# Closing attention by a transposed reciprocal, and a new cost model in the instruction planner, in a hybrid RWKV-7 / gMLP / attention backbone

## The chip, the cores and the metric

One Trainium2 chip, one core. The metric is the device time of one launch in microseconds, the median of several runs. The engines are TensorE (PE, with PEld for its weight loads), VectorE (DVE), ScalarE (ACT), GpSimd (POOL) and SyncE (SP, which issues the DMAs).

## The reference

Two layers over 512 latent tokens and 256 context tokens of width 1024. In each layer one input projection feeds three groups of heads (RWKV-7 in two directions, a chunked spatial gate, grouped-query attention with 6 query heads), one output projection and a SwiGLU follow, each with adaLN modulation and a gated residual. What the change rewrites is the end of the attention:

```python
def _attend(q, keys, vals):
    s = jnp.einsum('bqhgd,bkhd->bhgqk', q, keys).astype(jnp.float32) * (HEAD_DIM ** -0.5)
    p = jax.nn.softmax(s, axis=-1).astype(vals.dtype)
    return jnp.einsum('bhgqk,bkhd->bqhgd', p, vals)
...
    o = lax.map(lambda qblk: _attend(qblk, k_all, v_all), qb)
    ...
    if need_ctx_out:
        ...
        oc = _attend(qc, kc, vc).reshape(qc.shape[:2] + (C_W,))
    ...
    x = x + g1 * (jnp.concatenate([oA, oB, oC], axis=-1) @ w_out)
    x = x + g2 * swiglu(modulate(rmsnorm(x, n2), sh2, sc2), w1, w2)
```

The context queries (`oc`) exist in the first layer only. Everything is float32. The scan of the RWKV heads and the attention don't depend on each other; both end in the concatenation before `w_out`.

## The kernel before

Activations lie with the channels on the partitions and the tokens along the free dimension. Matrices are split into a high and a low part, and a product is three matmuls. Each layer has an input part (norm, 20 chunks of the input projection), a **planned part** (the method `rwkv`) and a feed-forward part. In the profile the planned part of the first layer runs from about 263 to 745 us, that of the second from about 1472 to 1900 us.

In the planned part nine generators run side by side: `scan(0)` and `scan(1)` (the recurrences, 9 units of 4 chunks each in either direction), `stage2` (inverses, by `inverse`), `solve` (a substitution on POOL between two DMAs), `back`, `front` (preparing units), `pairs`, `post` (the output norm of the RWKV heads) and `project`. `project` runs the whole attention first, then the output projection (tiles `o_ps`). `interleave` draws the next step from the generator that the planner's running clock puts earliest, which fixes the order of emission and with it the order in which buffers of a ring are handed out.

When all is emitted, `Planner.order` sorts the instructions anew. `graph` builds the dependencies, `cost` gives every instruction a duration and a lag (`late`), `HOPS` the delay from engine to engine. `run` is a list scheduler with priorities, run forward and backward in turn for `ROUNDS` rounds with the settings in `WEIGHTS`; it also guesses when TensorE's clock is halved (`active`, `ACTIVE`, `slow`). The round with the shortest modelled span wins, and its order is written into PE, DVE, ACT and POOL as a chain of dependencies, so each of these engines runs its instructions strictly in that order. SP is not ordered. `cost` puts a DVE instruction at 69 ns and 1.04 ns for each column (reciprocals too), and an ACT one that reads PSUM at 50 ns and 0.85 ns for each column.

Attention works by items: 6 heads of 512 latent queries, and in the first layer also 6 heads of 256 context queries, so 12 items and then 6. Of an item, `att_max` finds bounds of the scores, `att_scores` makes one block of transposed scores (`st_ps`, in the PSUM ring "as" of two buffers) and its exponentials (`p`, in a ring of one buffer, and `ph`), `att_rest` their low part `pl`, and `att_weigh` adds the block's product with the values to `o` (tile `at_ps`, a ring of one). The values stand beside 64 columns of ones, so `o` holds the output in one half of the partitions and the sum of the exponentials, repeated 64 times, in the other. `att_close` divides:

```python
        y = self.mix[5 + it["j"]][pr, q0:q0 + nq]
        self.nc.vector.reciprocal(out=y, in_=o[op, :nq])
        self.tt(y, o[pr, :nq], y, ALU.mult)
```

The next item's first product can't enter `at_ps` until both have read it.

Of the kernel before, what the change touches and what calls it, by code (L numbers as in the profile page):

```python
# [8 lines left out]
F32 = mybir.dt.float32  # L9
F32R = mybir.dt.float32r  # L10
AF = mybir.ActivationFunctionType
ALU = mybir.AluOpType
# [6 lines left out]
TL = 512  # L19
# [23 lines left out]

WEIGHTS = ((60.0, 0.0), (60.0, 0.15), (20.0, 0.15), (120.0, 0.3), (20.0, 0.4), (8.0, 0.15))
DRAIN = (0.10, 0.14)
ACTIVE = 3400
TICK = 10.24 / 3
SOON = 3.0
ROUNDS = 40
LATE = (0.0, 0.0, 0.4, 0.2, 0.6, 0.3, 0.5, 0.4, 1.0)  # L50


ENGINES = ("PE", "DVE", "Activation", "Pool", "SP")

HOPS = {("Activation", "PE"): 0.25, ("DVE", "PE"): 0.23, ("PE", "Activation"): 0.2, ("PE", "DVE"): 0.2,
        ("DVE", "Activation"): 0.13, ("Activation", "DVE"): 0.15, ("Activation", "Pool"): 0.17, ("DVE", "Pool"): 0.12,
        ("Pool", "Activation"): 0.08, ("Pool", "DVE"): 0.08, ("Pool", "PE"): 0.2, ("PE", "Pool"): 0.22}

# [12 lines left out]
class Planner:  # L71
# [25 lines left out]
    def cost(self, i, e):  # L97

        out = i.outs[0].bass_ap
        n = 1  # L100
        for _, k in out.ap[1:]:
            n *= k
        ins = [a.bass_ap for a in i.ins if hasattr(a, "bass_ap")]
        late = 0.0
        if e == "PE":
            m, rows = out.ap[0][1], ins[0].ap[0][1]
            low = out.offset // out.ap[0][0] == 0
            dur, occ, load, passes = n / 2.4, 0.0, m / 1.2, 1
            if i.is_transpose:
                dur, load, passes = dur * 2, load / 2, 2  # L110
            elif i.ins[0].dtype == F32:
                dur, passes = dur * 4, 4
                if not low or rows <= 64 < m:
                    dur, late = dur / 2, dur / 2
                if low:
                    occ = m / 1.2

            shape = tuple(32 if x <= 32 else 64 if x <= 64 else 128 for x in (rows, m))
            self.parts[i.name] = (dur + 2) / 1e3, (occ + 2) / 1e3, load / 1e3, n * passes * rows / 128, shape
            c = max(dur, occ + load) + 2  # L120
        elif e == "DVE":
            kind = type(i).__name__
            wide = len([a for a in ins if len(a.ap) > 2 or a.ap[-1][1] > 1])
            if kind == "InstTensorReduce":
                for _, k in ins[0].ap[1:]:
                    n *= k
                c = 40 + 1.04 * n
            elif kind == "InstMemset" or kind in ("InstTensorScalarPtr", "InstTensorCopy") and wide < 2 and \
                    not any(a.tensor.name in self.psum for a in ins):
                c = 69 + 0.52 * n  # L130
            else:
                c = 69 + 1.04 * n + (60 if len(ins) > 2 else 0)
        elif e == "Activation":
            c = (50 if ins[0].tensor.name in self.psum else 57) + 0.85 * n + 95 * (len(ins) - 1)
        elif e == "Pool":
            if str(getattr(i, "op", "")).endswith("pow"):
                c = 400 + 165 * n
            elif not ins:
                c = 130 + 0.85 * n
            else:  # L140
                c = 250 + 2.1 * n if n > 100 else 260 + 1.65 * n
        else:
            c = 2700 + (0.6 * n if out.ap[0][1] == 128 else 0)
        return c / 1e3, late / 1e3
# [95 lines left out]
    def order(self):  # L240

        ins = [i for i in self.bb.instructions[self.from_:] if i.is_executable and len(i.outs)]
        eng = [str(i.engine).split(".")[-1] for i in ins]
        n = len(ins)
        deps, data, ready = self.graph(ins, eng)
        cost, late = zip(*[self.cost(i, e) for i, e in zip(ins, eng)])
        parts = [self.parts.get(i.name) for i in ins]

        def lag(j, k):
            if eng[j] == eng[k] and eng[j] in ("DVE", "Activation"):  # L250
                return 0.12 if j in data[k] else 0.0
# [8 lines left out]
        def run(prio, back, weight=(60.0, 0.0)):  # L260

            wait_w, stay = weight
            pre, suc = (succ, pred) if back else (pred, succ)
            left = [len(p) for p in pre]
            at = [0.0] * n if back else list(ready)
# [5 lines left out]
            start, seq = [0.0] * n, []  # L271
            loaded, active, shape, end = 0.0, {}, None, 0.0
            while len(seq) < n:
# [5 lines left out]
                if e == "PE" and not back:  # L279
# [4 lines left out]
                    drain = DRAIN[slow > 1.0]  # L284

                    def delay(k):
                        if parts[k][4] == shape:
                            return max(0.0, loaded + slow * parts[k][2] - t)
                        return max(0.0, end + drain - t) + slow * parts[k][2]

                    k = max(av, key=lambda k: prio[k] - wait_w * delay(k))
                    if stay and parts[k][4] != shape:

                        soon = [r for r, x in pend[e] if r < t + stay and parts[x][4] == shape and prio[x] > prio[k] - wait_w * stay]
                        if soon:
                            free[e] = min(soon)
                            continue
                    dur, occ, load, cols, form = parts[k]
                    if form != shape:
                        t = max(t, end + drain)  # L300
                        f = t + slow * (load + dur)
                    else:
                        t = max(t, loaded + slow * load)
                        f = t + slow * dur
                    loaded, end, shape = t + slow * occ, f, form
                    active[int(f / TICK)] = active.get(int(f / TICK), 0.0) + cols
                else:
# [24 lines left out]
            return start, seq, max(free.values())  # L332

        prio = [0.0] * n
# [50 lines left out]
class Kern:  # L385
# [323 lines left out]
    def attention(self, pool, psp, tn):  # L709
# [12 lines left out]
        for n, _ in enumerate(items):  # L722
# [1111 lines left out]
```

## Time and profile before

| what | us |
|---|---|
| median of 3 runs | 2278.98 (2271.74 to 2285.78) |
| the profiled execution's own time | 2289.83 |
| its span, first to last instruction | 2288.1 |
| planned part, layer 0 (263 to 745) | 482 |
| feed-forward, layer 0, with the norm before it (745 to 1307) | 562 |
| planned part, layer 1 (1472 to 1900) | 428 |
| feed-forward, layer 1, and the end (1900 to 2288) | 388 |

The profiled execution is 10.9 us above the median and 1.7 us longer than its span. The rest of the span is the two input parts. The stretches were cut by hand where the first and last instructions of a part lie, so neighbours overlap a little.

### The profile page before, as it was taken

The numbers are of one execution on the slowest core, as the hardware profiler recorded it, in microseconds if no ns is written. First come the engines' busy times: TensorE is split into PE (matmuls) and PEld (weight loads), VectorE is DVE, ScalarE is ACT, GpSimd is POOL, SyncE is SP. The second block draws the span as 40 slices with busy tenths as digits, with TensorE's granted clock in tenths as the row PEclk, the third lists the DMA queues.
The fourth block names the chain that finished last, engine by engine and source line by source line (L and its number), as shares of the span: only waits on it lengthen the run. The fifth ranks groups of instructions, "written<-read, shape, count | busy, mean of one in ns | idle before, by whom it ended". The sixth has DMA issues, their size and how long they took to land.

```text
span 2288.1 us, 37945 instructions
## 1 busy us (share of the span) xinstructions
PE 2109.2 (92%) x15184; PEld 1718.6 (75%) x15184; DVE 1343.8 (59%) x2362; ACT 871.9 (38%) x1822; POOL 475.7 (21%) x965
## 2 busy tenths in 40 slices
PE   6989988888999899999999899979888898999997
PEld 2778765666788788888888778756666777888886
DVE  3677787778646744296354464477786646333334
ACT  3534355564544421121121254336555444222221
POOL 0123372444311100000000012363534401000000
PEclk9999887987699899999999999977898898999998
DMA  7433010001211423256253231011111212323322
GB/s 262 144 119 121 30 28 10 16 19 27 61 50 36 145 92 89 68 175 191 77 175 114 100 97 56 28 21 18 23 28 30 74 49 75 101 92 96 97 91 76
DMA packets 128928, 183.05 MB, mean 80 GB/s; under 512 B 82032, under 2 KB 85360, under 8 KB 128752
## 3 DMA queue, kind: packets, MB, share of 16 engines
q1 hardware_dynamic: 128752, 180.63, 26.0%
q8 instruction: 119, 1.95, 0.4%
q14 instruction: 57, 0.47, 0.1%
HBM read 168.93 MB, written 11.67 MB: 79 GB/s over the span
## 4 chain that ended last, share of the span: by engine, by line
PE 65%; DVE 8%; ACT 4%; issue 2%; DMA 1%; POOL 1%; POOLq 0%; SPq 0%; DVEq 0%; ACTq 0%
PE pgate L413 26%; PE p L413 14%; PE g_ps L413 6%; PE o_ps L413 5%; PE sc_ps L413 4%; PE st_ps L413 2%; PE at_ps L413 1%; DVE mix L822 1%; PE pe L413 1%; DVE BK L406 1%; DVE sz L406 1%; ACT XU L400 1%; PE pT L413 1%; PE pa_ps L413 1%; PE pD L413 1%
## 5 line engine op out<-in xcount | busy, mean ns | idle before, releaser
L400 ACT ACTIVATE whi<-wraw 128x1024 fp32r<-128x1024 f32 (+1 forms) x192 | 198.2, 1033 | 727.7 <-issue 260.3
L413 PE MATMUL pgate<-h2l,whi 128*128 128x512 f32 (+1 forms) x1056 | 376.5, 357 | 4.0 <-DVE h2l L406 4.0
L413 PE MATMUL pgate<-h2h,whi 128*128 128x512 f32 (+1 forms) x1056 | 375.2, 356 | 4.2 <-ACT h2h L400 3.2
L413 PE MATMUL pgate<-h2h,wlo 128*128 128x512 f32 (+1 forms) x1056 | 376.6, 357 | 0.0
L403 DVE TENSOR_TENSOR wlo<-wraw,whi 128x1024 fp32r<-128x1024 f32 (+1 forms) x192 | 231.9, 1208 | 188.3 <-ACT whi L400 176.1
L413 PEld LDWEIGHTS pgate<-h2h,whi 128*128 128x128 f32 x1056 | 199.9, 189 | 37.2 <-ACT h2h L400 4.0
L413 PEld LDWEIGHTS pgate<-h2l,whi 128*128 128x128 f32 x1056 | 199.7, 189 | 37.2 <-DVE h2l L406 5.4
L413 PEld LDWEIGHTS pgate<-h2h,wlo 128*128 128x128 f32 x1056 | 199.6, 189 | 28.7
L403 POOL TENSOR_TENSOR rs<-ms,consts_sb 128x4 f32<-128x4 f32 (+2 forms) x51 | 71.8, 1407 | 671.0 <-DVE ms L410 613.9
L413 PE MATMUL g_ps<-hh,whi 128*128 128x512 f32 (+1 forms) x552 | 193.7, 357 | 12.0 <-ACT hh L400 7.4
L413 PE MATMUL g_ps<-hl,whi 128*128 128x512 f32 (+1 forms) x552 | 195.7, 355 | 1.0 <-POOL hl L403 1.0
L413 PE MATMUL g_ps<-hh,wlo 128*128 128x512 f32 (+1 forms) x552 | 194.2, 352 | 0.0
L413 PE MATMUL p<-tL,whi 128*128 128x512 f32 (+1 forms) x528 | 186.8, 355 | 0.0
L413 PE MATMUL p<-tH,wlo 128*128 128x512 f32 (+1 forms) x528 | 186.4, 356 | 0.0
L413 PE MATMUL p<-tH,whi 128*128 128x512 f32 (+1 forms) x528 | 186.0, 354 | 0.0
L488 DVE CUSTOM_DVE_ANT_0 ada_junk<-adaw,cb,glob 128x1024 bf16<-128x1024 f32 x128 | 165.6, 1294 | 29.7 <-DMA adaw<-in_ada_w 28.1
L406 DVE SCALAR_TENSOR_TENSOR part<-p,adav,part 128x512 f32<-128x512 f32 (+1 forms) x72 | 47.5, 661 | 179.2 <-PE p L413 179.2
L406 DVE SCALAR_TENSOR_TENSOR fe<-fe,pgate 128x768 f32<-128x768 f32 (+1 forms) x88 | 71.9, 818 | 130.1 <-PE pgate L413 129.9
L413 PEld LDWEIGHTS g_ps<-hh,whi 128*128 128x128 f32 x552 | 105.7, 193 | 30.6 <-ACT hh L400 9.5
L400 ACT ACTIVATE sw<-sz,wc 64x64 f32<-64x64 f32 x264 | 90.9, 344 | 95.0 <-DVE sz L406 75.4
L413 PEld LDWEIGHTS g_ps<-hl,whi 128*128 128x128 f32 x552 | 107.1, 194 | 16.9 <-issue 2.5
L413 PEld LDWEIGHTS g_ps<-hh,wlo 128*128 128x128 f32 x552 | 106.8, 194 | 13.6 <-issue 0.6
(282 smaller groups left out, 4262.9 us busy)
## 6 DMA issues: line engine op xcount, KB each, us to landing
wraw<-in_w SPq DMA_DIRECT2D x104, 512.0 KB, 3.4
adaw<-in_ada_w SPq DMA_DIRECT2D x80, 512.0 KB, 3.7
wraw<-in_w_in SPq DMA_DIRECT2D x40, 512.0 KB, 3.7
wraw<-in_w SPq DMA_DIRECT2D x32, 448.0 KB, 3.3
adar<-in_ada_r SPq DMA_DIRECT2D x16, 512.0 KB, 8.2
wraw<-in_w_out SPq DMA_DIRECT2D x16, 448.0 KB, 3.3
drA<-EA SPq DMA_DIRECT2D x72, 64.0 KB, 2.1
Z<-drY SPq DMA_DIRECT2D x36, 128.0 KB, 3.1
```

Source lines behind the costliest of these rows:

```text
L400: self.lastact = self.nc.scalar.activation(out=out, in_=in_, func=func, **kw).ins
L403: (eng or self.nc.vector).tensor_tensor(out=out, in0=a, in1=b, op=op)
L406: self.lastdve = self.nc.vector.scalar_tensor_tensor(out=out, in0=a, scalar=s, in1=b, op0=op0, op1=op1).ins
L413: return self.nc.tensor.matmul(out=out, lhsT=lhsT, rhs=rhs, start=start, stop=stop, **kw)
L488: nc.vector.tensor_tensor_reduce(out=junk, in0=w, in1=self.cb[i], scale=1.0, scalar=self.adab[l][:, j:j + 1], op0=ALU.mult, op1=ALU.add, a ...
L822: self.nc.vector.reciprocal(out=y, in_=o[op, :nq])
```

## The change

Two things change, both inside the planned parts.

`att_close` becomes a generator of three steps. ACT copies all 128 partitions of `o` to SBUF (`ao`, which takes the one buffer of the ring "p"). TensorE transposes `ao` in blocks of 128 queries into `ot_ps` (ring "as"), so that queries lie on the partitions; VectorE takes the reciprocal of one column of each block, 128x4 or 128x2 numbers (`rc`); TensorE transposes these columns, spread over 128, back into `ob_ps` (ring "as"); VectorE multiplies `ao` by that. An item of 512 queries adds 8 transposes, one of 256 queries adds 4.

The planner gets other numbers and a second evaluation. `cost` now takes 150 ns or more for each DVE instruction and 165 or 198 ns for an ACT one, and books part of it as a lag where all 128 partitions are written; reciprocals and scans have their own slopes. `HOPS` are shorter, PE has a lag of 165 ns. PE is modelled as two halves, into which narrow matmuls go side by side in pairs. `follow` replays a finished order, engine by engine, with a clock model at three phases; a round is rated by the mean of the three spans, and priorities start from the replay. There are 100 rounds in place of 40.

```diff
-WEIGHTS = ((60.0, 0.0), (60.0, 0.15), (20.0, 0.15), (120.0, 0.3), (20.0, 0.4), (8.0, 0.15))
+WEIGHTS = ((60.0, 0.15), (20.0, 0.4), (10.0, 0.3), (120.0, 0.3), (30.0, 0.6), (8.0, 0.15), (4.0, 0.3))
 DRAIN = (0.10, 0.14)
-ACTIVE = 3400
+ACTIVE = 3600
+PHASES = (0.0, 0.33, 0.67)
 TICK = 10.24 / 3
 SOON = 3.0
-ROUNDS = 40
+ROUNDS = 100
 LATE = (0.0, 0.0, 0.4, 0.2, 0.6, 0.3, 0.5, 0.4, 1.0)
 
 
 ENGINES = ("PE", "DVE", "Activation", "Pool", "SP")
 
-HOPS = {("Activation", "PE"): 0.25, ("DVE", "PE"): 0.23, ("PE", "Activation"): 0.2, ("PE", "DVE"): 0.2,
-        ("DVE", "Activation"): 0.13, ("Activation", "DVE"): 0.15, ("Activation", "Pool"): 0.17, ("DVE", "Pool"): 0.12,
-        ("Pool", "Activation"): 0.08, ("Pool", "DVE"): 0.08, ("Pool", "PE"): 0.2, ("PE", "Pool"): 0.22}
+HOPS = {("Activation", "PE"): 0.052, ("DVE", "PE"): 0.054, ("PE", "Activation"): 0.037, ("PE", "DVE"): 0.038,
+        ("DVE", "Activation"): 0.033, ("Activation", "DVE"): 0.033, ("Activation", "Pool"): 0.077, ("DVE", "Pool"): 0.078,
+        ("Pool", "Activation"): 0.033, ("Pool", "DVE"): 0.034, ("Pool", "PE"): 0.053, ("PE", "Pool"): 0.08}
 
 
 def overlap(a, b):
...
         ins = [a.bass_ap for a in i.ins if hasattr(a, "bass_ap")]
+        full = out.ap[0][1] == 128
+        psum = any(a.tensor.name in self.psum for a in ins)
         late = 0.0
         if e == "PE":
             m, rows = out.ap[0][1], ins[0].ap[0][1]
-            low = out.offset // out.ap[0][0] == 0
-            dur, occ, load, passes = n / 2.4, 0.0, m / 1.2, 1
+            dur, load, times = n / 2.33 + 8, m / 1.2, 1
+            passes = 1
             if i.is_transpose:
-                dur, load, passes = dur * 2, load / 2, 2
+                dur, passes = n / 1.2, 2
             elif i.ins[0].dtype == F32:
-                dur, passes = dur * 4, 4
-                if not low or rows <= 64 < m:
-                    dur, late = dur / 2, dur / 2
-                if low:
-                    occ = m / 1.2
-
+                dur, passes, times = n / 1.2 + (5 if m <= 64 else 0), 4, 2
+
+            half = None if m > 64 else int(out.offset // out.ap[0][0] >= 64)
             shape = tuple(32 if x <= 32 else 64 if x <= 64 else 128 for x in (rows, m))
-            self.parts[i.name] = (dur + 2) / 1e3, (occ + 2) / 1e3, load / 1e3, n * passes * rows / 128, shape
-            c = max(dur, occ + load) + 2
+
+            self.parts[i.name] = dur / 1e3, times, load / 1e3, n * passes * rows / 128, shape, half
+            c = max(dur, load) * times
+            if half is not None:
+                c *= 0.55
+            late = 165.0
         elif e == "DVE":
             kind = type(i).__name__
             wide = len([a for a in ins if len(a.ap) > 2 or a.ap[-1][1] > 1])
             if kind == "InstTensorReduce":
                 for _, k in ins[0].ap[1:]:
                     n *= k
-                c = 40 + 1.04 * n
-            elif kind == "InstMemset" or kind in ("InstTensorScalarPtr", "InstTensorCopy") and wide < 2 and \
-                    not any(a.tensor.name in self.psum for a in ins):
-                c = 69 + 0.52 * n
+                c = 150 + 1.04 * n
+            elif kind == "InstReciprocal":
+                c = 160 + 6.25 * n
+            elif getattr(i, "is_tensor_tensor_scan", False):
+                c = 150 + 2.1 * n
+            elif kind == "InstMemset" or kind in ("InstTensorScalarPtr", "InstTensorCopy") and wide < 2 and not psum:
+                c = 150 + 0.52 * n + 55 * (len(ins) - 1)
             else:
-                c = 69 + 1.04 * n + (60 if len(ins) > 2 else 0)
+                c = 150 + 1.04 * n + (60 if len(ins) > 2 else 0)
+            c, late = (c - 83, 83) if full else (c + 12, 0)
         elif e == "Activation":
-            c = (50 if ins[0].tensor.name in self.psum else 57) + 0.85 * n + 95 * (len(ins) - 1)
+            c = (165 if psum else 198) + 0.845 * n + 90 * (len(ins) - 1)
+            c, late = (c - 93, 93) if full else (c + 14, 0)
         elif e == "Pool":
             if str(getattr(i, "op", "")).endswith("pow"):
-                c = 400 + 165 * n
+                c, late = 400 + 165 * n, -60
             elif not ins:
-                c = 130 + 0.85 * n
+                c, late = 145 + 0.84 * n, -55
             else:
-                c = 250 + 2.1 * n if n > 100 else 260 + 1.65 * n
+                c, late = 270 + 1.9 * n, -70
         else:
-            c = 2700 + (0.6 * n if out.ap[0][1] == 128 else 0)
+            c = 2600 + (0.6 * n if full else 0)
         return c / 1e3, late / 1e3
...
         def lag(j, k):
-            if eng[j] == eng[k] and eng[j] in ("DVE", "Activation"):
-                return 0.12 if j in data[k] else 0.0
+            if eng[j] == eng[k] != "SP":
+                return max(0.0, late[j]) + 0.033 if j in data[k] and eng[j] in ("DVE", "Activation") else 0.0
             return self.hop(eng[j], eng[k]) + late[j]
...
+            weights, ends = [0.0, 0.0], [0.0, 0.0]
+            active, shape = {}, None
+
+            def place(k, t, drain, slow):
+
+                dur, times, load, _, form, half = parts[k]
+                hs = (0, 1) if half is None else (half,)
+                t = max([at[k], t] + [weights[h] for h in hs])
+                if form != shape:
+                    t = max(t, max(ends) + drain)
+                t = max([t + slow * load] + [ends[h] for h in hs])
+                last = t + (times - 1) * slow * max(dur, load)
+                return t, last + slow * dur, last, hs
+
+            def occupy(k, drain, slow, t):
+                t, f, last, hs = place(k, t, drain, slow)
+                for h in hs:
+                    weights[h], ends[h] = last, f
+                tick = int(f / TICK)
+                active[tick] = active.get(tick, 0.0) + parts[k][3]
+                return t, f
+
...
+                    issue = max(0.0, t - 0.25)
+                    k = max(av, key=lambda k: prio[k] - wait_w * (place(k, issue, drain, slow)[0] - t))
                     if stay and parts[k][4] != shape:
 
                         soon = [r for r, x in pend[e] if r < t + stay and parts[x][4] == shape and prio[x] > prio[k] - wait_w * stay]
                         if soon:
                             free[e] = min(soon)
                             continue
-                    dur, occ, load, cols, form = parts[k]
-                    if form != shape:
-                        t = max(t, end + drain)
-                        f = t + slow * (load + dur)
-                    else:
-                        t = max(t, loaded + slow * load)
-                        f = t + slow * dur
-                    loaded, end, shape = t + slow * occ, f, form
-                    active[int(f / TICK)] = active.get(int(f / TICK), 0.0) + cols
+                    half = parts[k][5]
+                    both = [k]
+                    if half is not None:
+
+                        mate = [x for x in av if parts[x][4] == parts[k][4] and parts[x][5] == 1 - half]
+                        if mate:
+                            both.append(max(mate, key=lambda k: prio[k]))
+                    f = t
+                    for x in both:
+                        start[x], fx = occupy(x, drain, slow, issue)
+                        shape = parts[x][4]
+                        f = max(f, fx)
+                        av.remove(x)
+                        seq.append(x)
+                    free[e] = f
+                    for k in both:
+                        for x, l in suc[k]:
+                            if eng[x] != "PE":
+                                at[x] = max(at[x], f + l)
+                            left[x] -= 1
+                            if not left[x]:
+                                heapq.heappush(pend[eng[x]], (at[x], x))
+                    continue
...
+        def follow(seq, phase):
+
+            rows = {e: [k for k in seq if eng[k] == e] for e in ENGINES}
+            nxt, free = dict.fromkeys(ENGINES, 0), dict(self.free0)
+            left, at = [len(p) for p in pred], list(ready)
+            rows["SP"] = []
+            weights, ends = [0.0, 0.0], [0.0, 0.0]
+            active, shape, slow = {}, None, 1.0
+            start, span = [0.0] * n, 0.0
+            able = []
+
+            def offer(e):
+                if nxt[e] < len(rows[e]):
+                    k = rows[e][nxt[e]]
+                    if not left[k]:
+                        heapq.heappush(able, (max(free[e], at[k]), k))
+
...
         best = None
         for i in range(ROUNDS):
-            start, seq, span = run(prio, False, WEIGHTS[i % len(WEIGHTS)])
+            _, seq, _ = run(prio, False, WEIGHTS[i % len(WEIGHTS)])
+            trace = [follow(seq, ph * TICK) for ph in PHASES]
+            span = sum(s for _, s in trace) / len(trace)
             if best is None or span < best[1]:
                 best = seq, span
+            start = trace[i % len(trace)][0]
             start, _, _ = run([t + c for t, c in zip(start, cost)], True)
             prio = [t + c for t, c in zip(start, cost)]
...
-            self.att_close(o, cur)
-            yield
+            yield from self.att_close(pool, psp, o, cur)
...
-    def att_close(self, o, it):
+    def att_close(self, pool, psp, o, it):
+
         hf, nq, q0 = it["hf"], it["nq"], it["q0"]
-        pr, op = slice(hf * 64, hf * 64 + 64), slice(64 - hf * 64, 128 - hf * 64)
-        y = self.mix[5 + it["j"]][pr, q0:q0 + nq]
-        self.nc.vector.reciprocal(out=y, in_=o[op, :nq])
-        self.tt(y, o[pr, :nq], y, ALU.mult)
+        pr, nb = slice(hf * 64, hf * 64 + 64), nq // 128
+        ao = pool.tile([128, TL], F32, name="ao", tag="p")
+        self.act(ao[:, :nq], o[:, :nq])
+        yield
+        tp = psp.tile([128, 4, 128], F32, name="ot_ps", tag="as", bufs=2)
+        for b in range(nb):
+            self.tr(out=tp[:, b, :], in_=ao[:, b * 128:(b + 1) * 128], identity=self.ident)
+        rc = pool.tile([128, 4], F32, name="rc", tag="rc")
+        self.nc.vector.reciprocal(out=rc[:, :nb], in_=tp[:, :nb, 64 - 64 * hf])
+        yield
+        bc = psp.tile([128, TL], F32, name="ob_ps", tag="as", bufs=2)
+        for b in range(nb):
+            self.tr(out=bc[:, b * 128:(b + 1) * 128], in_=rc[:, b:b + 1].to_broadcast([128, 128]), identity=self.ident)
+        self.tt(self.mix[5 + it["j"]][pr, q0:q0 + nq], bc[pr, :nq], ao[pr, :nq], ALU.mult)
+        yield
```

## Rows read from the trace of the kernel before

**Rows 1.** The page's first part: busy us, share of the span, instructions.

```profile
PE 2109.2 (92%) x15184; PEld 1718.6 (75%) x15184; DVE 1343.8 (59%) x2362; ACT 871.9 (38%) x1822; POOL 475.7 (21%) x965
```

**Rows 2.** Busy time by stretch: planned parts, their ends, feed-forward parts.

```profile
core 0: us, PE busy (x) PEld busy (x) DVE busy (x) ACT busy (x) POOL busy (x), PEclk, DMA share, GB/s
263.00:745.00 482.00, 428.25 (x4400) 339.98 (x4398) 343.03 (x739) 241.98 (x656) 186.90 (x450) 0.84 0.13 30
1472.00:1900.00 428.00, 366.49 (x3899) 281.15 (x3897) 296.79 (x646) 220.54 (x609) 173.14 (x432) 0.84 0.15 32
745.00:1307.00 562.00, 555.13 (x3173) 481.77 (x3174) 294.65 (x384) 127.36 (x145) 7.69 (x4) 0.99 0.38 122
...
600.00:745.00 145.00, 139.84 (x1602) 122.63 (x1600) 78.29 (x201) 59.26 (x172) 38.54 (x85) 0.94 0.18 48
1772.00:1900.00 128.00, 108.85 (x1278) 93.56 (x1278) 75.12 (x175) 58.31 (x163) 30.84 (x67) 0.89 0.20 57
...
1900.00:2288.00 388.00, 370.54 (x1600) 302.57 (x1600) 160.95 (x187) 104.64 (x131) 6.90 (x5) 0.97 0.29 92
```

**Rows 3.** The page's chain that ended last, by engine and by line.

```profile
PE 65%; DVE 8%; ACT 4%; issue 2%; DMA 1%; POOL 1%; POOLq 0%; SPq 0%; DVEq 0%; ACTq 0%
PE pgate L413 26%; PE p L413 14%; PE g_ps L413 6%; PE o_ps L413 5%; PE sc_ps L413 4%; PE st_ps L413 2%; PE at_ps L413 1%; DVE mix L822 1%; PE pe L413 1%; DVE BK L406 1%; DVE sz L406 1%; ACT XU L400 1%; PE pT L413 1%; PE pa_ps L413 1%; PE pD L413 1%
```

**Rows 4.** Groups on DVE and ACT by shape: busy us, mean ns, idle before.

```profile
L822 DVE RECIPROCAL mix<-at_ps 64x512 f32<-64x512 f32 x12 | 40.3, 3355 | 1.5 <-PE at_ps L413 1.1
L822 DVE RECIPROCAL mix<-at_ps 64x256 f32<-64x256 f32 x6 | 10.5, 1755 | 1.5 <-PE at_ps L413 1.3
L403 DVE TENSOR_TENSOR pl<-p,ph 128x512 fp32r<-128x512 f32 x78 | 57.4, 735 | 20.8 <-ACT ph L400 9.8 <-PE at_ps L413 9.0 <-ACT rz L400 0.5
L403 DVE TENSOR_TENSOR mix<-at_ps,mix 64x512 f32<-64x512 f32 x12 | 8.2, 685 | 0.2
L403 DVE TENSOR_TENSOR mx<-mx 128x4 f32<-128x4 f32 x12 | 2.0, 166 | 0.1
L1076 DVE COPY XU<-sc_ps 64x64 f32<-64x64 f32 x144 | 31.6, 219 | 21.3 <-PE sc_ps L413 18.8 <-POOL Z L1011 0.7
L400 ACT ACTIVATE ph<-p 128x512 fp32r<-128x512 f32 x78 | 49.0, 628 | 1.9
L400 ACT ACTIVATE p<-st_ps 128x512 f32<-128x512 f32 x78 | 46.5, 596 | 73.1 <-PE st_ps L413 41.4 <-DVE pl L403 16.4 <-PE pe L413 6.7
L400 ACT ACTIVATE XU<-sc_ps 64x64 f32<-64x64 f32 x144 | 31.2, 217 | 33.8 <-PE sc_ps L413 32.5
```

**Rows 5.** Busy by stretch: each of 18 reciprocals and 0.7 us behind it.

```profile
323.88:327.94 4.06, 2.88 (x51) 2.20 (x49) 4.02 (x3) 2.42 (x6) 2.72 (x9) 1.00 0.14 32
...
1772.74:1776.79 4.05, 2.91 (x43) 2.72 (x44) 4.02 (x2) 3.94 (x10) 2.45 (x9) 0.50 0.01 3
sum 63.39, PE 35.43 PEld 27.34 DVE 62.48 ACT 29.80 POOL 20.99; mean PE 1.97 PEld 1.52 DVE 3.47 ACT 1.66 POOL 1.17
```

**Rows 6.** Timeline around one reciprocal: start, us, instruction, idle before.

```profile
478.28 3.36 DVE L822 RECIPROCAL mix<-at_ps 64x512 f32<-64x512 f32 x1
...
481.68 0.68 DVE L403 TENSOR_TENSOR mix<-at_ps,mix 64x512 f32<-64x512 f32 x1
...
482.50 0.47 PE L413 MATMUL at_ps<-ph,vh 128*128 128x512 f32 x1 [1.76 <-DVE mix L403]
```

**Rows 7.** Timeline of TensorE: groups of four and of two transposes.

```profile
304.52 0.60 PE L416 MATMUL pb<-consts_sb,BK 128*128 128x128 f32 x4
1536.83 1.11 PE L416 MATMUL pb<-consts_sb,BK 128*128 128x128 f32 x4
1679.48 0.38 PE L416 MATMUL pb<-consts_sb,BK 128*128 128x128 f32 x2
1537.74 0.63 PE L416 MATMUL bc_ps<-consts_sb,nkk 128*128 128x128 f32 x2
```

**Rows 8.** Tile at_ps in either layer: min/median/max ns, first and last start.

```profile
L413 PE MATMUL at_ps<-ph,vh x48: 277/415/796, 298.7 to 574.7; 128*128 128x512 f32 x36, 128*128 128x256 f32 x12
L413 PE MATMUL at_ps<-ph,vh x36: 387/439/797, 1503.7 to 1767.7; 128*128 128x512 f32 x36
```

**Rows 9.** Timeline of TensorE: a stretch with transposes alone.

```profile
746.53 1.54 PE L416 MATMUL nbc<-consts_sb,rs 128*128 128x128 f32 x6 [1.67 <-POOL rs L403]
```

**Rows 10.** Busy time in that stretch, columns as in rows 2.

```profile
746.20:748.20 2.00, 1.54 (x6) 1.14 (x6) 0.09 (x1) 1.06 (x1) 0.28 (x1) 0.50 0.91 324
```

**Rows 11.** The chain in order of time, near the end of layer 1's planned part.

```profile
1772.74 3.35 DVE mix L822
1776.12 0.70 DVE ml L403
...
1799.93 2.15 DMA drA<-EA
1802.20 2.66 DMA FM<-drA
...
1818.24 4.20 DMA wraw<-in_w_out
```

More of the change, by code (lines that the diff above doesn't have):

```diff
@@ L271, in run @@
             start, seq = [0.0] * n, []
-            loaded, active, shape, end = 0.0, {}, None, 0.0
+            weights, ends = [0.0, 0.0], [0.0, 0.0]
[16 more added lines that the diff above has]
+                return t, f
             while len(seq) < n:
@@ L284, in run @@
                     drain = DRAIN[slow > 1.0]
[L286 to L291, printed above, removed]
+                    issue = max(0.0, t - 0.25)
+                    k = max(av, key=lambda k: prio[k] - wait_w * (place(k, issue, drain, slow)[0] - t))
                     if stay and parts[k][4] != shape:
@@ L332, in run @@
             return start, seq, max(free.values())
+        def follow(seq, phase):
[12 more added lines that the diff above has]
+                        heapq.heappush(able, (max(free[e], at[k]), k))
+            for e in ENGINES:
+                offer(e)
+            for k in range(n):
+                if eng[k] == "SP" and not left[k]:
+                    heapq.heappush(able, (at[k], k))
+            while able:
+                t, k = heapq.heappop(able)
+                e = eng[k]
+                start[k] = t
+                if e == "PE":
+                    dur, times, load, cols, form, half = parts[k]
+                    hs = (0, 1) if half is None else (half,)
+                    t = max([t] + [weights[h] for h in hs])
+                    tick = int((max([t] + ends) + phase) / TICK)
+                    slow = 1.0 if tick < 1 or active.get(tick - 1, 0.0) > ACTIVE else 2.0
+                    if form != shape:
+                        t = max(t, max(ends) + DRAIN[slow > 1.0])
+                        shape = form
+                    free[e] = t + 0.006
+                    t = max([t + slow * load] + [ends[h] for h in hs])
+                    last = t + (times - 1) * slow * max(dur, load)
+                    f = last + slow * dur
+                    for h in hs:
+                        weights[h], ends[h] = last, f
+                    x, y = t + phase, f + phase
+                    w, z = int(x / TICK), int(y / TICK)
+                    for v in range(w, z + 1):
+                        active[v] = active.get(v, 0.0) + cols * (min(y, (v + 1) * TICK) - max(x, v * TICK)) / (y - x)
+                else:
+                    f = t + cost[k]
+                    if e != "SP":
+                        free[e] = f
+                span = max(span, f)
+                for x, l in succ[k]:
+                    if e != "PE" or eng[x] != "PE":
+                        at[x] = max(at[x], f + l)
+                    left[x] -= 1
+                    if not left[x]:
+                        q = eng[x]
+                        if q == "SP":
+                            heapq.heappush(able, (at[x], x))
+                        elif q != e and rows[q][nxt[q]] == x:
+                            heapq.heappush(able, (max(free[q], at[x]), x))
+                if e != "SP":
+                    nxt[e] += 1
+                    offer(e)
+            return start, span
```

## Prediction

> **What bounds the kernel now.** I began with the busy shares. TensorE is busy 92% of the span, VectorE 59% [rows 1], which says little, because the kernel has parts with different limits. The table by stretch separates them [rows 2]: in the feed-forward parts TensorE is busy 96 to 99% of the time at a granted clock of 0.97 to 0.99, and the change doesn't touch them. The two planned parts last 482 and 428 us, 910 together. There TensorE is busy 428.3 and 366.5 us (87%), VectorE 343.0 and 296.8 us (70%), ScalarE 242.0 and 220.5 us (51%), and the clock is 0.84 on the mean. So these parts have no single bound: TensorE is the fullest engine, but it stands idle 115 us and runs part of its work at the lower of its two levels (1.2 GHz where 2.4 is full). With a mean of 0.84, the share at the lower level is (1 - 0.84) x 2 = 32%, or 291 us; at 87% busy, 254 us of TensorE's time lie there, which would take 127 us at the full level.
>
> The chain that ended last shows the reciprocals by name: "DVE mix L822", rounded to 1% of the span [rows 3]. The groups by shape give their cost: 12 of 3355 ns and 6 of 1755 ns, 50.8 us [rows 4], by far the longest single instructions on VectorE.
>
> **What a reciprocal blocks.** I measured the 18 stretches of a reciprocal and the 0.7 us of its multiplication behind it: 63.4 us, of which TensorE was busy 35.4 us, or 56% [rows 5]. At the planned parts' 87% it would have been 55.3. So the long instruction starves TensorE of about 20 us beyond the ordinary idling; all its idle time there is 28 us. One case in order of time shows how [rows 6]: the reciprocal starts at 478.28, the multiplication at 481.68, and only after that can the next item's product enter the buffer, at 482.50, with TensorE idle for 1.76 us.
>
> **The close of attention, step by step.** Removed: 50.8 us of VectorE. Added on VectorE: 18 reciprocals of 128x4 or 128x2. No row has one. The two shapes give a slope of (3355 - 1755) / 256 = 6.25 ns a column and 155 ns of fixed cost, so 4 columns take about 0.18 us (the nearest row of that shape, a minimum of 128x4, took 0.17 [rows 4]): 3.2 us in all. VectorE's multiplication stays at 0.69 us. Net on VectorE 47.6 us less, which is 5 points of its 70%.
>
> Added on ScalarE: 18 copies. The nearest row is the exponential out of PSUM, 596 ns for 128x512 [rows 4]; 12 of these and 6 of about 0.36 (a half in columns and the fixed part) are 9.3 us. ScalarE is at 51%, so I cost this at nothing; without that cover it is at most the 9.3.
>
> Added on TensorE: 24 groups of four transposes and 12 of two, 120 in all. Four took 0.60 us at the upper level and 1.11 at the lower, two 0.38 and 0.63 [rows 7]. The difference of two to four leaves out the start of a group: 0.11 us for one, or 0.24. So 120 x 0.11 = 13 us at one end, 29 at the other; end to end with their starts, all at the lower level, 24 x 1.11 + 12 x 0.63 = 34. With 32% at the lower level I take 0.68 x 13.2 + 0.32 x 28.8 = 18 us, since TensorE usually has other work queued behind a group.
>
> On the path: 20 us of starving go, 18 us of transposes come. At one place the chain itself is VectorE's, the last item of layer 1, where 3.35 us at 1772.74 stand ahead of the splits for the output projection [rows 11]; there VectorE's 3.2 us count in full. Sum: -20 + 18 - 3 = -5 us, with ends of -28 + 13 - 3 = -18 and -20 + 34 = +14. The close by itself thus moves little: it trades a starved TensorE for a busier one.
>
> **The waits that it adds.** `ao` takes the single buffer of `p`. The first exponential of the next item therefore waits until the final multiplication has read `ao`; on ScalarE's queue everything planned behind that exponential (the scans' `rz`, `XU` and `sw`) waits with it. `ot_ps` and `ob_ps` use both buffers of the ring "as", so the next item's scores start only when `rc` is taken. In exchange `at_ps` is free after one copy of 0.6 us, no longer after 4.0. I cost this at nothing because attention has slack: the first layer's 42 blocks (6 of them short) spread over 276 us and the second's 36 over 264 [rows 8], some 7 us for a block, whose own steps on ScalarE and VectorE (`p` 0.60, `ph` 0.63, `pl` 0.74 [rows 4]) are 2 us. What it costs without that slack is the rival below. No DMA is added.
>
> **The planner.** Nothing is removed; every instruction of the planned parts may move. The old costs are checked against rows. A 64x64 copy on VectorE was planned at 69 + 1.04 x 64 = 136 ns and took 219; on ScalarE 50 + 0.85 x 64 = 104 ns against 217; an exponential 485 against 596; a reciprocal 601 against 3355 [rows 4]. The shortfall is about 0.08 us for each of VectorE's 1385 instructions and 0.11 for each of ScalarE's 1265 [rows 2]: 115 and 140 us of work, and 41 us of reciprocals, that the plan thought free. The new costs give 229, 233, and 505 plus a lag of 93, close to the rows. The old delays between engines hid much of this for the latency of a chain, not for how full an engine is. So the old plan filled VectorE and ScalarE too densely, and TensorE, which keeps a strict order, waited at the head of its queue.
>
> What a better plan is worth no row shows; it can be bounded. The room is the idle time outside the reciprocals, 115 - 28 = 87 us, and the 127 us that the lower clock costs: 214. The list scheduler, the dependencies and the strict queues stay, and the two plans of the old planner differ among themselves by 88.9 against 85.6% busy, 3.3 points, or 30 us on 910: that much comes or goes by luck, so the loss end is +30. The gain end I put at half the room, -107. I take a fifth of the room, -43, a little more than that luck, because the cost errors are large, the winner is the best of 100 replays and the replay has TensorE's clock in it. This is the least certain term. The replanning moves what SP's DMAs wait for as well: its queue is not ordered by the planner, and the substitution sits between two DMAs, whose landings (2.15 and 2.66 us at 1800) and a weight load at 1818 are on the chain [rows 11]; these I leave as they are.
>
> **The sum.** On the profiled execution 2289.8 - 5 - 43 = 2242; it lies 10.9 above the median of three, so against the median 2279.0 - 48 = **2231 us**. The case's own range is a tenth to 35% of the room: 2253 to 2199.
>
> **Rivals.**
> (a) The plan comes out much better: half the room, 2279 - 5 - 107 = 2167. For it: in the last 128 us of layer 1's part TensorE still idles 19, and the chain there goes through DMAs, which an earlier start of the last unit would hide [rows 2, 11]. Against: in the last 145 us of layer 0's part it idles only 5, and the clock is at 0.94 [rows 2]. The Trainium skill, "Perfetto Trace Analysis", section "Identifying the Most-Contended Engine", says that weight-load time and not matmul busy time shows TensorE's headroom; with 340 of 482 and 281 of 428 us [rows 2] the room would be 289 us of idle in place of 115.
> (b) The new plan is only another throw: nothing but the close counts, 2279 - 5 = 2274. For it: a list schedule reshuffled by other costs need not be shorter on the chip, and the replay leaves SP's queue free of order.
> (c) Slower: the close becomes the wait. From the last product to the next item's first `ph` the path was 4.0 us of division with `p` and `ph` hidden beside it; now it is 0.60 + 0.60 + 0.18 + 0.60 + 0.69 + 0.60 + 0.63 = 3.9 at the upper clock and 4.9 at the lower, with six handoffs through strict queues in place of two. At 0.3 us for a handoff (half an instruction of 0.6) that is 5.7 to 6.7 against 4.6, or about 2 us for each of 18 items: +36, no gain from the plan as attention ends the part, 2279 - 5 + 36 = 2310. It decides from the point where attention has no slack, as near the end of layer 1, where its close is on the chain now [rows 11].
> (d) Transposes don't hold the clock up. The only stretch with transposes alone ran at 0.50 [rows 10], but TensorE had been idle 1.67 us just before [rows 9], so it decides nothing. If 120 more of them bring the mean clock from 0.84 to 0.82, 36 us more run at the lower level, of which 31 are TensorE's work, and half of that, 16 us, is lost: 2231 + 16 = 2247. The Trainium skill, "TensorE: Matmul & The Clock Gate", section "Part 4: PE-mode transpose", states this rule; the planner, old and new, counts a transpose as full work. By the rule it would overrate the clock after each close.
>
> **Chances.** Forecast 0.50, (a) 0.15, (b) 0.17, (c) 0.12, (d) 0.06. The measurement tells about 1% (23 us) from no change: the three runs of before spread over 14 us. Faster by over 1% are the forecast, (a) and half of (d): 0.68; within 1% (b) and the other half of (d): 0.20; slower (c): 0.12. The range for 8 in 10 runs from 2165, which leaves out the better half of (a), to 2292, which leaves out most of (c).
>
> **What would show it.** Right: the two planned parts together 860 us or so in place of 910, VectorE's busy time there down by some 48 us, TensorE's idle time in them under 100, a mean clock above 0.84, feed-forward parts unchanged to 2 us. The close: no stretch on VectorE of over 2 us at an item's end, groups of four transposes at 0.6 to 1.1 us. For (b): VectorE down, but the parts as long. For (c): the first exponential of an item waiting on the multiplication by `ao`, long in the list of waits, and attention's last product later than 312 us after the first layer's part begins (574.7 - 263) and 296 after the second's [rows 8]. For (d): the clock down in the stretches of the closes. I am wrong most likely in the planner's term, in either direction.

## The result, and the profile after

The changed kernel takes 2210.9 us, the median of four runs (2204.2 to 2212.8), against 2282.4 (2271.7 to 2287.0) before: 71 us less, a ratio of 0.9688 with a 95% interval of 0.9646 to 0.9730. The forecast was 48 us less. The profiled execution took 2204.2 us, the lowest of its runs, and that of before 2289.8, above all of its own, so the two traces differ by 85.6 us, more than the medians do.

All of it lies in the planned parts. Busy time by stretch, columns as in [rows 2]: the planned parts of layer 0 and layer 1, then the two feed-forward parts. In every trace the planned part of layer 0 is cut from the first instruction on the attention's queries (`qs`) to the norm's sums (`nst`) that end it, that of layer 1 from 162.2 us behind the sums that end the first feed-forward part to the sums that end it. In the trace of before this cut gives 480.2 and 426.8 us.

```profile
261.30:683.60 422.30, 383.06 (x4459) 301.87 (x4459) 312.96 (x737) 244.18 (x667) 197.75 (x450) 0.95 0.14 34
1412.60:1814.30 401.70, 361.26 (x3954) 277.97 (x3953) 276.03 (x646) 225.33 (x617) 170.75 (x431) 0.85 0.16 35
...
685.30:1247.30 562.00, 555.41 (x3173) 481.77 (x3173) 294.40 (x384) 127.34 (x145) 7.67 (x4) 0.99 0.38 121
1815.40:2202.40 387.00, 369.16 (x1600) 301.39 (x1600) 161.17 (x187) 104.51 (x131) 6.86 (x5) 0.97 0.29 93
```

The planned parts are 57.9 and 25.1 us shorter; the feed-forward parts, 562 and 387 us, are as long as in [rows 2]. In layer 0 the granted clock rose from 0.84 to 0.95, and TensorE's busy time fell by 44 us although it runs 72 transposes more; its idle time is 39 us. In layer 1 the clock hardly moved and the idle time fell from 61 to 40.

VectorE and ScalarE by shape, to be held against [rows 4]:

```profile
L511 DVE TENSOR_TENSOR mix<-ob_ps,ao 64x512 f32<-64x512 f32 x12 | 8.2, 685 | 1.9 <-PE ob_ps L524 1.5 <-ACT vr L508 0.2
L936 DVE RECIPROCAL rc<-ot_ps 128x4 f32<-128x4 f32 x12 | 2.1, 175 | 0.4 <-PE ot_ps L524 0.2
L936 DVE RECIPROCAL rc<-ot_ps 128x2 f32<-128x2 f32 x6 | 1.0, 166 | 1.3 <-PE ot_ps L524 1.3
...
L508 ACT ACTIVATE ao<-at_ps 128x512 f32<-128x512 f32 x12 | 7.2, 597 | 1.2 <-PE at_ps L521 0.9
L508 ACT ACTIVATE ao<-at_ps 128x256 f32<-128x256 f32 x6 | 2.3, 383 | 1.4 <-PE at_ps L521 1.3
```

The 50.8 us of reciprocals became 3.1, and ScalarE gained 9.5. One close in order of time, where [rows 6] showed a reciprocal:

```profile
419.95 0.60 ACT L508 ACTIVATE ao<-at_ps 128x512 f32<-128x512 f32 x1
...
420.61 0.66 PE L524 MATMUL ot_ps<-consts_sb,ao 128*128 128x128 f32 x4
...
421.70 0.18 DVE L936 RECIPROCAL rc<-ot_ps 128x4 f32<-128x4 f32 x1
...
422.50 0.65 PE L524 MATMUL ob_ps<-consts_sb,rc 128*128 128x128 f32 x4
...
423.25 0.68 DVE L511 TENSOR_TENSOR mix<-ob_ps,ao 64x512 f32<-64x512 f32 x1 [0.16 <-PE ob_ps L524]
```

From the copy to the end of the multiplication it takes 4.0 us, as long as the division and its multiplication had taken, but none of the steps holds an engine for more than 0.7 us. Of attention's products the first and last start, as in [rows 8], are now

```profile
L521 PE MATMUL at_ps<-ph,vh x48: 278/394/628, 288.1 to 530.3; 128*128 128x512 f32 x36, 128*128 128x256 f32 x12
L521 PE MATMUL at_ps<-ph,vh x36: 387/438/628, 1459.6 to 1670.1; 128*128 128x512 f32 x36
```

so attention spreads over 242 and 211 us in place of 276 and 264.

### The profile page after: what moved, and what is told of

It is laid out like the page before. It is cut to its first block, busy times and chain, and to the rows that moved or that the text cites. A ratio compares the mean times of both kernels' runs of the same rounds, so it can differ in the third digit from the quotient of the medians.

```text
span 2202.4 us, 38243 instructions
## 1 busy us (share of the span) xinstructions
PE 2056.9 (93%) x15304; PEld 1675.3 (76%) x15304; DVE 1296.3 (59%) x2362; ACT 878.1 (40%) x1840; POOL 485.9 (22%) x965
```

## The experiments

My theory at the start was that of the prediction: the planner gives nearly all, the close about breaks even. The rival: the close gives half or more. The table has every run but e11, a single execution of 2226.4 us made for its trace. Each ratio is to the kernel before, run on the same chip beside it. "Another throw" is another order that the same planner writes when a small thing in its search is changed. The lengths and clocks are those of the planned parts in the profile, cut as above.

| run | planner | close | median us | ratio (95%) | layer 0 us, clock | layer 1 us, clock |
|---|---|---|---|---|---|---|
| before | old | old | 2282.4 | 1 | 480.2, 0.84 | 426.8, 0.84 |
| e12 | old, another throw | old | 2277.3 | 0.9958 (0.9924 to 0.9993) | 472.0, 0.85 | 426.7, 0.82 |
| e15 | old, same order | copy for reciprocal | 2235.9 | 0.9803 (0.9744 to 0.9862) | 444.7, 0.88 | 412.6, 0.86 |
| e2 | old | new | 2245.4 | 0.9836 (0.9794 to 0.9878) | 447.9, 0.91 | 415.0, 0.86 |
| e13 | old, another throw | new | 2238.9 | 0.9817 (0.9773 to 0.9861) | 446.8, 0.91 | 410.1, 0.87 |
| e1 | new | old | 2237.2 | 0.9793 (0.9739 to 0.9848) | 449.6, 0.86 | 400.8, 0.83 |
| e4 | old with new costs | new | 2225.8 | 0.9769 (0.9715 to 0.9823) | 444.8, 0.90 | 398.8, 0.87 |
| e3 | new with old costs | new | 2240.5 | 0.9824 (0.9780 to 0.9867) | 459.0, 0.87 | 402.1, 0.84 |
| after | new | new | 2210.9 | 0.9688 (0.9646 to 0.9730) | 422.3, 0.95 | 401.7, 0.85 |
| e7 | new, other phases | new | 2192.1 | 0.9616 (0.9555 to 0.9677) | 414.1, 0.95 | 393.9, 0.87 |
| e5 | new without replay | new | 2195.4 | 0.9612 (0.9561 to 0.9663) | 428.9, 0.91 | 380.5, 0.89 |
| e8 | new | new, other ring | 2185.2 | 0.9592 (0.9538 to 0.9647) | 422.3, 0.92 | 395.4, 0.84 |
| e6 | new without clock model | new | 2173.5 | 0.9531 (0.9481 to 0.9581) | 411.9, 0.96 | 381.3, 0.88 |

**e1, the planner alone.**

```diff
-        ao = pool.tile([128, TL], F32, name="ao", tag="p")
-        self.act(ao[:, :nq], o[:, :nq])
...
+        self.nc.vector.reciprocal(out=y, in_=o[op, :nq])
+        self.tt(y, o[pr, :nq], y, ALU.mult)
+        yield
```

> The changed kernel with the old close of attention (a reciprocal of 64x512 on VectorE), the new planner kept. Theory (nearly all of the 71 us comes from the planner; the close trades about 20 us of starving for 18 us of transposes): 2215 to 2230 us, and the first planned part still near 430 us. Rival (freeing 48 us of VectorE is what lets the plan close up): 2245 us or more.

Measured 2237.2 us, between the two; the first planned part took 449.6 us, not 430. The planner without the close gives 44 us, and the close on top of it 26 more.

**e2, the close alone.** The old planner with the new `att_close`.

> The kernel before with the new close alone, the old planner kept. Theory: 2265 to 2285 us, within 1% of before. Rival (the close gives half or more): 2250 us or less. A second rival (the single buffer of p makes the close the wait): over 2300 us.

Measured 2245.4 us: half of the gain with nothing of the planner. Theory and second rival fall, the rival holds. Its planned parts:

```profile
260.80:708.70 447.90, 404.42 (x4459) 320.34 (x4457) 311.55 (x738) 243.79 (x668) 188.27 (x450) 0.91 0.14 32
1440.90:1855.90 415.00, 363.82 (x3952) 285.72 (x3952) 277.26 (x646) 224.91 (x617) 176.32 (x431) 0.86 0.15 33
```

**e12 and e13, two other throws.** In a list scheduler any edit reshuffles everything, so 36 us could be luck of the order. In both kernels the settings of the rounds were taken from the second entry on:

```diff
-            start, seq, span = run(prio, False, WEIGHTS[i % len(WEIGHTS)])
+            start, seq, span = run(prio, False, WEIGHTS[(i + 1) % len(WEIGHTS)])
```

> The kernel before, its planner taking the settings of its rounds from the second entry on: another throw of the old planner with the old close. Theory (throws of one planner differ by some 20 us, the two changes are real): 2265 to 2300 us. Rival (the order of before was an unlucky one): 2255 us or less.

> The kernel before with the new close alone, and the rounds' settings from the second entry on. Theory (the close alone is worth some 25 to 35 us because VectorE is freed of work that no plan can hide): 2235 to 2260 us, at least 15 us under the other throw of the kernel before. Rival (the 36 us of the first trial were luck of the order): 2270 us or more.

2277.3 and 2238.9 us: the old planner's two throws lie 5 to 7 us apart with either close, and the close is worth 36 us in one pair and 38 in the other. With two throws each, luck of the order doesn't explain it.

**e15, the same order with shorter instructions.**

```diff
-        self.nc.vector.reciprocal(out=y, in_=o[op, :nq])
+        self.nc.vector.tensor_copy(y, o[op, :nq])
```

> The kernel before with each of the 18 reciprocals of attention replaced by a copy of the same tile, so the sums multiply where they should divide (the division is left out). The old planner gives a copy the same cost, so the order on PE, DVE, ACT and POOL in the planned parts stays as it was and only the duration changes: 12 x (3.36 - 0.69) + 6 x (1.76 - 0.42) = 40 us less on VectorE, and no transposes. Theory (while a reciprocal runs, most of what the strict queues hold waits for it, not TensorE's excess idling alone): 28 to 40 us faster, 2242 to 2255. Rival (the prediction's 20 us of starving are all): 2260 to 2268.

Measured 2235.9 us, 43 less than the 2279.0 of before beside it, 31 to 58 by the ratio's interval: all the 40 us taken off VectorE came back within the noise, and the prediction's 20 us are excluded. PE, DVE, ACT and POOL issue the planned parts' instructions in the order of before; only a few weight splits and matmuls of a feed-forward part and two of SP's DMAs stand elsewhere. The reciprocals' lines and the planned parts in this kernel:

```profile
L822 DVE COPY mix<-at_ps 64x512 f32<-64x512 f32 x12 | 8.3, 688 | 1.2 <-PE at_ps L413 0.8
L822 DVE COPY mix<-at_ps 64x256 f32<-64x256 f32 x6 | 2.5, 422 | 1.5 <-PE at_ps L413 1.3
```

```profile
260.40:705.10 444.70, 405.84 (x4389) 321.40 (x4387) 318.13 (x738) 241.12 (x656) 189.99 (x450) 0.88 0.13 32
1433.70:1846.30 412.60, 363.44 (x3902) 279.24 (x3901) 281.12 (x645) 221.70 (x610) 176.41 (x431) 0.86 0.15 34
```

and, cut the same way, in the kernel before:

```profile
263.10:743.30 480.20, 426.59 (x4388) 338.40 (x4387) 342.76 (x738) 241.88 (x656) 186.90 (x450) 0.84 0.13 30
1472.00:1898.80 426.80, 366.10 (x3898) 280.85 (x3897) 296.63 (x645) 220.54 (x609) 172.60 (x431) 0.84 0.15 33
```

These four lines say where the time went, since TensorE has the same work in the same order in both. Its idle time (length less busy) fell from 53.6 to 38.9 and from 60.7 to 49.2 us, 26 together. Its busy time fell from 426.6 to 405.8 and from 366.1 to 363.4, 23.4 together, for the same matmuls, with the granted clock up from 0.84 to 0.88 and 0.86. The two halves add up to nearly 50 us, 7 more than the medians differ, since the profiled execution of before was a long one (2289.8 us, mean clock 0.921). Among the runs of before the longer ones have the lower clock, from 2272.3 us at 0.932 to 2297.4 at 0.919 over the whole program, so the excess probably lies in the second half.

**e4 and e3, the planner cut in two.** e4 has the new close, the old planner, and only the new costs of DVE, ACT, POOL and SP with their delays; e3 has all that is new but these.

```diff
-                c = 69 + 1.04 * n + (60 if len(ins) > 2 else 0)
+                c = 150 + 1.04 * n + (60 if len(ins) > 2 else 0)
+            c, late = (c - 83, 83) if full else (c + 12, 0)
...
-            c = (50 if ins[0].tensor.name in self.psum else 57) + 0.85 * n + 95 * (len(ins) - 1)
+            c = (165 if psum else 198) + 0.845 * n + 90 * (len(ins) - 1)
```

> The kernel before with the new close and, of the planner, only the new costs of VectorE, ScalarE, GpSimd and SP with the delays between engines; the old model of TensorE, the old settings and 40 rounds stay. Theory (true costs of the small instructions are the planner's gain): 2205 to 2225 us. Rival (the model of TensorE in two halves is): 2240 us or more, as with the close alone.

> The changed kernel with the old costs of VectorE, ScalarE, GpSimd and SP and the old delays; TensorE's new model, the replay and 100 rounds stay. Theory (the costs are the gain): 2235 to 2255 us. Rival (TensorE's model, replay and rounds are): 2195 to 2215 us.

2225.8 us, just outside the theory's band, and 2240.5, inside it. With the new close and nothing else the time was 2245.4 and 2238.9; so true costs alone give 13 to 20 us, TensorE's new model, the replay and 100 rounds alone give nothing that can be told from a throw, and both together give 28 us or more. As far as one order of each can show, the second half pays only when it works on true costs.

**e5, e7 and e6: replay, phases, clock model.**

```diff
-            _, seq, _ = run(prio, False, WEIGHTS[i % len(WEIGHTS)])
-            trace = [follow(seq, ph * TICK) for ph in PHASES]
-            span = sum(s for _, s in trace) / len(trace)
+            start, seq, span = run(prio, False, WEIGHTS[i % len(WEIGHTS)])
...
-            start = trace[i % len(trace)][0]
```

> The changed kernel whose rounds are rated and steered by the list scheduler's own span, without the replay at three phases; costs, halves of TensorE and 100 rounds stay. Theory (the replay picks orders that hold on the chip): 2230 to 2250 us. Rival (true costs are enough): 2205 to 2220 us.

```diff
-PHASES = (0.0, 0.33, 0.67)
+PHASES = (0.15, 0.48, 0.82)
```

> The changed kernel with the replay at the phases 0.15, 0.48 and 0.82 in place of 0, 0.33 and 0.67: another throw of the same planner. Theory (the gain is systematic): 2200 to 2225 us. Rival (a lucky order): 2235 us or more, which would say that one throw differs from the next by over 1%.

```diff
-                    slow = 1.0 if tick == 0 or active.get(tick - 1, 0.0) > ACTIVE else 2.0
+                    slow = 1.0
...
-                    slow = 1.0 if tick < 1 or active.get(tick - 1, 0.0) > ACTIVE else 2.0
+                    slow = 1.0
```

> The changed kernel whose planner takes TensorE's clock as full all the time, in the list scheduler and in the replay. Theory (costs and halves carry the gain): 2190 to 2220 us. Rival (the clock model is what lifts the first planned part's clock from 0.84 to 0.95): 2225 us or more, and a clock there of 0.88 or less.

All three are faster than the changed kernel, and faster than either side had expected: 2195.4, 2192.1 and 2173.5 us. The replay isn't needed, against my theory. Other phases alone moved the time by 19 us, so the changed kernel's own order is one of the poorer throws. A planner that knows nothing of the clock wrote the fastest kernel of all, 4.7% under before, with an interval (0.9481 to 0.9581) below that of the changed kernel and below e7's median ratio of 0.9616; its planned parts:

```profile
261.30:673.20 411.90, 381.19 (x4459) 301.03 (x4458) 312.96 (x737) 243.57 (x667) 193.61 (x450) 0.96 0.14 34
1405.60:1786.90 381.30, 354.27 (x3967) 276.04 (x3967) 276.28 (x648) 226.54 (x619) 177.28 (x432) 0.88 0.16 36
```

The clock granted to it, 0.96 and 0.88, is higher than that of any plan with the clock model but e5's 0.89 in layer 1. That the clock model does harm isn't shown by one throw; that it isn't what lifted the clock is.

**e8, the wait on the ring.**

```diff
-        ao = pool.tile([128, TL], F32, name="ao", tag="p")
+        ao = pool.tile([128, TL], F32, name="ao", tag="ph", bufs=2)
```

> The changed kernel with the copy of the closed item in the ring of ph (two buffers) in place of that of p (one), so the next item's first exponential need not wait for the close. Theory (the wait costs little, 7.4 us of ScalarE's idle time in the changed kernel's trace): 2190 to 2215 us. Rival (the close has become the wait): 2180 us or less.

Inconclusive by its time: 2185.2 us, between the two bands and 7 us from e7, less than one throw differs from the next. The trace settles the wait itself. Who waited for the close's multiplication, in the changed kernel (us, times):

```profile
  ACT p L508: 7.4, 7
```

In e8 no exponential waits there. So the rival's wait existed and was 7.4 us of ScalarE's idle time; what it cost the kernel isn't shown, since e8's order differs too.

**e11, transposes and the clock.**

```diff
+                if last and k0 == PARTS[1][0]:
+                    tx = psp.tile([128, T], F32, name="tx_ps", tag="g", bufs=4)
+                    for _ in range(240):
+                        self.tr(out=tx[:, 0:128], in_=self.blk, identity=self.ident)
```

> The changed kernel with 240 transposes of a 128x128 constant put between the first and second third of the last layer's feed-forward part, where TensorE has been busy at full clock; their output is not used. If transposes hold the clock as matmuls do: granted clock 1.00 throughout, about 0.107 us each, 26 us in all. If they don't count: the clock falls to 0.50 within the stretch and the later ones take 0.21 us, 40 us or more in all.

Busy by stretch: ahead of the transposes, their first and second half, behind them.

```profile
1930.00:1950.40 20.40, 20.40 (x90) 16.73 (x90) 6.90 (x7) 3.19 (x3) 0.00 (x0) 1.00 0.29 103
...
1950.40:1963.00 12.60, 12.60 (x116) 12.48 (x115) 1.98 (x2) 1.06 (x1) 0.00 (x0) 1.00 0.12 43
1963.00:1976.80 13.80, 13.80 (x130) 13.80 (x128) 0.00 (x0) 0.00 (x0) 0.00 (x0) 1.00 0.01 1
1976.80:1990.00 13.20, 13.20 (x60) 10.86 (x59) 3.61 (x4) 3.13 (x4) 0.00 (x0) 1.00 0.13 42
```

240 transposes took 26.4 us, 0.11 us each, at a clock of 1.00 to the end. The Trainium skill, "TensorE: Matmul & The Clock Gate", section "Part 4: PE-mode transpose", says that full clock doesn't engage for transposes, because they don't count as busy in the same way; in this trace they held it, at least as float32 transposes behind dense matmuls. Whether transposes can raise the clock from the lower level no run shows.

## Why the prediction was right, and where its sum was not

The direction and the range held: 2210.9 lies in 2165 to 2292. The planned parts came to 824 us where 860 were forecast, VectorE's busy time there is 50 us less where 48 were, TensorE's idle time 80 where under 100 was, the feed-forward parts moved by 0 and 1 us.

**The planner's term was about right, in part by luck.** Forecast -43; measured -44 with the old close (e1) and -34.5 with the new (2245.4 to 2210.9). The forecast was a judgement, a fifth of the room, and the changed kernel's order is one throw: with the new close e7's order would have given -53. Its reason, costs that are too small for short instructions, is borne out by e4 and e3, but not alone: the costs without the rest give 13 to 20 us. Which of the rest matters I can't say fully. Without the replay (e5) or the clock model (e6) the gain stays, in one order each; that leaves the rest of TensorE's new model (its two halves, costs and lag), the settings and the number of rounds, which weren't tried apart. "The replay has TensorE's clock in it" was a wrong reason.

**The close was mis-sized: forecast -5, measured -36 and -38 with the old planner, -26 with the new.** The step that failed is "What a reciprocal blocks". It took only TensorE's idle time beyond the ordinary in the 18 stretches, 20 us. e15 changes nothing but those instructions' length and measures 43 us, in two halves that its lines show (their sum is that of two profiled executions, 7 us above what the medians give): 26 us of idle time, where I had 20, and 23.4 us of matmul time at the lower clock, which I had left out of this step altogether, though the room that I worked out for the planner had 127 us of the same kind in it. The clock in layer 0 rose from 0.84 to 0.88 with the order unchanged, so the starving itself had kept it down. By the plain count of VectorE, 40 us removed in a part where it was 70% busy, the answer would have been nearer.

**The price of the transposes stays open.** Forecast 18 us. The new close (e2) is 9.5 us slower than the copy (e15), or 7.4 with each taken against the kernel before beside it, and the intervals of the two ratios overlap. That difference holds the transposes, the copy by ScalarE and the added waits, but also a saving: e15 has 10.8 us of copies on VectorE where the new close has 3.1 us of reciprocals. If these 7.7 us count at their length, as e15's 40 did, the additions cost about 15 to 17 us, an estimate near the forecast. The trace of the changed kernel has TensorE busy with them for 22.8 us, overlaps with neighbouring matmuls included:

```profile
L524 PE MATMUL ob_ps<-consts_sb,rc 128*128 128x128 f32 x60 | 11.6, 295 | 0.7 <-DVE rc L936 0.7
L524 PE MATMUL ot_ps<-consts_sb,ao 128*128 128x128 f32 x60 | 11.2, 296 | 0.0
```

In layer 0 TensorE is busy about as long in e2 as in e15 (404.4 and 405.8 us) with 72 transposes more, at a granted clock of 0.91 against 0.88. What raised the clock there no run separates from the order.

**The rivals.** (a) Half the room was not reached by this change. e6 is 105 us under the kernel before beside it, near the 112 of that rival, but some 36 of these are the close's; its planner gave about 72 (2245.4 to 2173.5), a third of the room of 214. (b) fell, as the close counts for more and the planner's gain stands in e1; its warning holds in part, since the new planner's throws (after, e7, and e5, e8, e6 with other edits) lie between 2174 and 2211. (c) fell: the wait is in the trace, at 7.4 us, and attention ended sooner. (d) fell: with the transposes the clock in the planned parts rose, from 0.84 to 0.91 and 0.86 under the old planner (e2), and e11's transposes held it.

## What to carry to other kernels

A long instruction on a strictly ordered engine can cost about its length, as here at 70% busy, when the fullest engine's queue hangs on it: price the idle time that it causes downstream, and then the matmul time that runs at the lower clock because of that. To price it cleanly, put a short instruction in its place with the order held, as in e15. A planner's short instructions should be costed from the trace before its search is refined, and one order's time is a throw: compare planners over several.

## What the runs showed of the hardware

TensorE's time for unchanged work shrank by 20.8 us in layer 0 when VectorE's 12 long instructions there became short (e15, clock 0.84 to 0.88, one profiled execution of each kernel). Float32 transposes behind dense matmuls held the clock (e11, 1.00 over 26.4 us). A reciprocal's time went by its columns, not its numbers: 64x512 took 3355 ns [rows 4] and 128x4 took 175. The slope and fixed part read off the two old shapes give 180 for four columns; by the count of numbers, 512, they would give 205.
